# Small tiles of a hybrid block moved to GpSimd's DMA queue, with two kinds of PSUM banks and new latest chunks

## The chip, the cores and the metric

The kernel runs on one core of one Trainium2 chip. The metric is the device time of one execution in microseconds (us); smaller is better. Besides timed runs there is one profiled execution of the kernel, whose trace gives the rows that are shown. In it PE is the matrix engine (TensorE), PEld its weight loads, DVE is VectorE, ACT is ScalarE, POOL is GpSimd and SP is SyncE, which here does nothing but issue DMAs.

## The reference

One layer of a streaming-encoder block on 512 tokens of width 2048, all in f32. The normalised input feeds one wide projection, whose columns go to three branches and to gates; each branch is multiplied by a SiLU gate, projected back to 2048 columns, weighted by a sigmoid gate and summed; a last projection is added to the input.

```python
h = rms_norm(x, norm_g)
p = h @ w_in                       # all branches and gates
A = B * causal_conv3(C * u)        # 1024 channels
M = mla_attention(...)             # 16 heads, low-rank q and kv, rope, chunk mask
X = memory_attention(...)          # 4 heads over 256 memory tokens
A, M, X = A * silu(zA), M * silu(zM), X * silu(zX)
y = sig(gA) * (A @ w_conv_out) + sig(gM) * (M @ w_mla_out) + sig(gX) * (X @ w_mem_out)
return x + y @ w_o
```

## The kernel before

**Precision.** Each f32 operand is split into a rounded part and a remainder, hi and lo (`split`: the rounding is an ACT instruction, L129, the remainder a DVE subtraction, L131). A product is three matmuls, hi·hi, hi·lo and lo·hi (`mm3`, L160 to L162). Every weight is loaded raw (512 KB tiles), split into whi and wlo, and multiplied.

**Chunks.** After the attention of the MLA branch (which ends well before 690 us) the kernel is a written list, `plan`, of 504 chunks, each with one 512 KB weight tile's worth of matmuls (24 matmuls of 5.44 us by the plan's own cost, or 12 matmuls of 2.72 us, or 24 short ones of 2.88 us). The list in order: memory queries (8 chunks), the gate columns memz in two groups of 8, conv (8 groups of 14), mlaz and gconv (4 groups of 14 each), gmem and gmla (2 groups of 28 each), the projection mem_out (16), mla_out (2 groups of 28), the projection conv_out (16), and w_o (2 groups of 28). `plain_group` makes plain chunks; `block_group` and `block_group_t` make chunks of a seven-product scheme, where sums and differences of weight tiles (DVE, L1031, L1116, L1121) and of the tokens (`build`: sums, evens, forms, odds, with costs of 1.26, 0.69, 1.53 and 0.69 us) replace the eighth product. In `block_group_t` the products come in the order P1, P7, P5, P6 (four rounds), then four chunks of P4, then P2 and P3 in turn. The first group of w_o has an order of its own at its start. Results of a block are named "11", "10", "00" and "01".

**Order of work.** `drive` walks over the chunks and emits the instructions of ACT, DVE, PE and POOL in a fixed order: in chunk c first the hooks `at[c]` (mostly loads), then the sums and splits of the weights up to two or three chunks ahead, then the phases, then waiting pieces of work (`todo`), then the chunk's matmuls. A piece has a cost; it is emitted if the cost fits the `room` of DVE left in the chunk (with 0.3 us of grace, or 1.3 in the "patient" chunks, four before w_o and twelve into it), or if it has waited 3 chunks (12 in patient ones), or if its latest chunk, `by`, has come. What a chunk's result needs (`done`) is put into `todo` after its matmuls. Ahead of chunk 0 the order is a scheduler's.

**Buffers.** There are three sets of whi and wlo, so the split of a chunk's weights waits on ACT and DVE for the matmuls of the chunk three before. Raw tiles have four to ten slots. Results of gates and sums, 128x512 f32 (256 KB), live in the tile y, which has four buffers; `when` and `in_turn` load y tiles once one of the four is free by the written order.

**Queues.** SP issues the weight loads (raw: L903, L1070), the loads of the projections' inputs (araw, L1553), those of L1698, and all y loads (`y_tile`, L1212 to L1215, whose DMA is L1214), in one order. An issue that has to wait for a buffer holds up what stands behind it. ACT issues the stores. POOL issues the accumulating DMAs of `conv_result` (`add`, L1674), which add a gated projection (product on DVE, L1677) to a tile of the merged sum.

**PSUM.** The eight banks have four tags, aux0, aux1, acc0 and acc1, of two banks each. `take_pairs` hands out tags from the list `pairs` in turn; a group of four banks takes two tags. The first memz group has the fixed kind acc, so acc0 and acc1 by turns; the second memz group, which follows it, takes the first of the list. A bank can be written again once its result has been read: in memz by an ACT SiLU (L1338) in place and a DVE product (L1341); in mem_out by L1598; in mla_out by L1631 (sums), L1635 (gate), with L1641 (merge) behind it; in the transposes `turn_sums` by copies (L1720).

The steps of the projections: `load(c)` brings araw, `parts_` splits it into the tile act, and `group` makes the chunks and the y loads of the gates.

Of the kernel before, what the change touches and what calls it, by code (L numbers as in the profile page):

```python
# [94 lines left out]
def body(ctx, tc, a, out):  # L95
# [16 lines left out]
    psum = ctx.enter_context(tc.tile_pool(name="ps", bufs=2, space=bass.MemoryType.PSUM))  # L112
# [4 lines left out]
    turns = defaultdict(int)  # L117

    def bank_of(tag):
        return psum.tile([P, 512], F32, tag=tag, name=tag)  # L120

    def bank(tag):

        turns[tag] += 1
        return bank_of(f"{tag}{turns[tag] % 2}")
# [685 lines left out]
    def drive():  # L811
        n, npre, nprep, room = len(plan), 0, 0, 0.0
        for c in range(-3, n + 6):
# [4 lines left out]
            room = min(room, 0.0) + us  # L818
# [68 lines left out]
    def next_banks(n=4, tag=None):  # L887
        if tag is not None:
            return [bank(tag) for _ in range(n)]
        return [bank_of(t) for t in take_pairs(n // 2) for _ in range(2)]  # L890


    def plain_group(src, nch, kc, n, xs, early=4, lead=2, tag=None, mode="F"):


        banks = []
        first = len(plan)
        for c in range(nch):
            hold = {}

            def load(hold=hold, c=c):
                t = take_raw("W")[1].rearrange("p k n -> p (k n)")
                nc.sync.dma_start(t, src[c])  # L903
# [43 lines left out]
    def block_group(src, tokens, consume, loads=(-8, -7, -3, -2), add=None, halves=False):  # L947
# [70 lines left out]
        for n, ch in HALVES_ORDER if halves else PLAIN_ORDER:  # L1018
# [22 lines left out]
                def mm(ch=ch, bn=bn, xn=xn, hold=hold):  # L1041
                    opens = bn not in bk
                    if not bk:
                        bk["pairs"] = take_pairs(2)
                    if opens:
                        bk[bn] = bank_of(bk["pairs"]["XYZW".index(bn) // 2])
# [12 lines left out]
    def block_group_t(src, tokens, results, early=6, opening=()):  # L1059
# [48 lines left out]
        for name, ch in order:  # L1108
# [21 lines left out]
            def mm(name=name, ch=ch, bn=bn, xn=xn, hold=hold):  # L1130
                opens = bn not in bk
                if not bk:

                    bk["pairs"] = take_pairs(4)
                    pairs[:] = [bk["pairs"][i] for i in (3, 1, 0, 2)]
                if opens:
                    bk[bn] = [bank_of(bk["pairs"]["XYZW".index(bn)]) for _ in range(2)]
# [74 lines left out]
    def y_tile(src):  # L1212
        t = pres.tile([P, S], F32, tag="y", name="y", bufs=4)
        nc.sync.dma_start(t, src)  # L1214
# [281 lines left out]
    def gate_rows(n0, grp):  # L1496
# [3 lines left out]
        def results(name, o, i0, i1):  # L1500
# [23 lines left out]
            out_ = [(0, 0 if i1 is None else 0.69, piece(lambda tb=tb: made(tb), by=first + 29)) for tb in range(2)]  # L1524
# [15 lines left out]
    for n, nm in ((0, "w_gmem"), (2, "w_gmla")):  # L1540
        for grp in range(2):
            block_group_t(a[nm][grp], tx, gate_rows(16 * n, grp))


    def projection(weights_, n0, gate, result, halves=None, gates=None, mode="F"):
# [25 lines left out]
        def group(src, nch, kc, n, j):  # L1571
            g0, banks = plain_group(src, nch, kc, n, lambda k: acts[k], early=3, mode=mode)
# [12 lines left out]
        for grp in range(4):  # L1585
            if grp < 3 or halves is None:
                group(weights_[grp], 4, KC, 512, 4 * grp)
            else:
                for i in range(2):
                    group(halves[i], 2, 4, HS, 12 + 2 * i)  # L1590
# [3 lines left out]
    def mem_result(j, b, sg):  # L1594
# [3 lines left out]
        return [(0, 0.69, piece(lambda: vec.tensor_tensor(out=sg(), in0=b(), in1=sg(), op=ALU.mult), sg)),  # L1598
# [14 lines left out]
    def mla_rows(grp):  # L1613
# [3 lines left out]
        def load(name, tb, k):  # L1617
            ys[name, tb, k] = y_tile((mdram if k else gdram[32:])[rows(grp, name, tb)])
# [4 lines left out]
        def results(name, o, i0, i1):  # L1623
            y = lambda tb, k: (lambda: ys.get((name, tb, k)))
            end = first + {"11": 20, "10": 28, "00": 29, "01": 30}[name]
            inx = o is not None
            out_ = []
            for tb in range(2):
# [25 lines left out]
            return out_ + [(3, 0, lambda tb=tb: store(tb)) for tb in range(2)]  # L1654
        return results

    for grp in range(2):
        block_group_t(a["w_mla_out"][grp], ta, mla_rows(grp), 6 if grp else 5)
# [29 lines left out]
    def turn_sums(n):  # L1688
# [41 lines left out]
    def out_group(grp, early):  # L1730
# [54 lines left out]
        block_group_t(a["w_o"][grp], to, results, early, () if grp else opening)  # L1785
# [107 lines left out]
```

## Time and profile before

| what | us |
|---|---|
| median of three timed runs | 2211.35 (2210.38 to 2215.31) |
| the profiled execution's own time | 2208.95 |
| its span in the profile | 2207.2 |
| PE busy | 2138.1 (97%) |
| DVE busy | 1574.5 (71%) |
| ACT busy | 1031.1 (47%) |
| POOL busy | 181.3 (8%) |

The span runs from the first to the last instruction of the trace. A row of a view names a line of the kernel, an engine, an operation and its tiles as "out<-in". PE is pipelined, and its busy time says nothing of its clock; the granted clock is listed by window as a share of full speed. The DMA engines moved 323.93 MB at a mean of 147 GB/s; the hardware queues are listed as q1 and q10, and the queue on which POOL's DMAs run as q0, with 8.39 MB.

### The profile page before, as it was taken

How to read it: one execution, taken by the hardware profiler on the slowest of the kernel's cores; microseconds unless marked ns; L12 is line 12 of the kernel's file. 1: busy time of each engine (PE TensorE's matmuls, PEld its weight loads, DVE VectorE, ACT ScalarE, POOL GpSimd, SP SyncE). 2: the span in 40 equal slices, each digit the busy share in tenths (PEclk: the TensorE clock that was granted, in tenths of full speed). 3: DMA queues.
4: the chain of work that ended last, by engine and by line, in shares of the span. 5: the costliest groups of instructions: out<-in, count | busy, mean ns of one | idle time of the engine just before them, and what ended most of it. 6: DMA issues, size and time to landing. Idle time of an engine off the chain costs nothing.

```text
span 2207.2 us, 31861 instructions
## 1 busy us (share of the span) xinstructions
PE 2138.1 (97%) x12504; PEld 1896.5 (86%) x12504; DVE 1574.5 (71%) x2194; ACT 1031.1 (47%) x1551; POOL 181.3 (8%) x157
## 2 busy tenths in 40 slices
PE   7999999999999999999999999999999999989899
PEld 5788888887778999999999999888888878878687
DVE  7853767774335887787777767777776779846887
ACT  5532677674333444444444544445444433424433
POOL 7510312220001000000000000000000000001000
PEclk9999999999999999999999999999999999999999
DMA  7473212134227523423345334335335746478352
GB/s 261 161 254 109 78 57 74 63 130 156 83 77 236 206 89 106 139 97 105 129 147 194 133 116 153 105 134 172 135 102 203 251 169 201 155 242 252 105 200 96
DMA packets 116103, 323.93 MB, mean 147 GB/s; under 512 B 13296, under 2 KB 13552, under 8 KB 115952
## 3 DMA queue, kind: packets, MB, share of 16 engines
q1 hardware_dynamic: 90000, 274.87, 36.6%
q10 hardware_dynamic: 21600, 38.63, 4.6%
q0 software_dynamic: 4352, 8.39, 2.0%
q8 instruction: 98, 1.61, 0.3%
q14 instruction: 53, 0.43, 0.1%
HBM read 269.41 MB, written 48.23 MB: 144 GB/s over the span
## 4 chain that ended last, share of the span: by engine, by line
PE 88%; DVE 5%; DMA 2%; ACT 2%; issue 2%; POOL 1%; ACTq 0%; SPq 0%; DVEq 0%; POOLq 0%
PE acc L161 16%; PE acc L160 16%; PE acc L162 16%; PE aux L161 12%; PE aux L160 12%; PE aux L162 12%; DVE wlo L154 1%; PE aux L211 1%; DVE wlo L131 1%; PE aux L667 1%; DMA raw<-in_w_conv_out 1%; ACT whi L129 1%; POOL xs L311 1%; PE aux L647 0%; PE aux L649 0%
## 5 line engine op out<-in xcount | busy, mean ns | idle before, releaser
L131 DVE TENSOR_TENSOR wlo<-raw,whi 128x1024 fp32r<-128x1024 f32 x440 | 538.4, 1224 | 377.5 <-ACT whi L129 364.6
L129 ACT ACTIVATE whi<-raw 128x1024 fp32r<-128x1024 f32 x440 | 465.9, 1060 | 689.0 <-PE acc L161 188.5
L154 DVE TENSOR_TENSOR wlo<-raw,whi 128x1024 fp32r<-128x1024 f32 (+3 forms) x97 | 119.1, 1229 | 105.3 <-ACT whi L153 104.1
L153 ACT ACTIVATE whi<-raw 128x1024 fp32r<-128x1024 f32 (+3 forms) x97 | 92.4, 953 | 124.9 <-PE acc L162 49.7
L160 PE MATMUL acc<-whi,blk 128*128 128x512 f32 (+1 forms) x320 | 120.7, 381 | 7.3 <-ACT blk L129 5.3
L161 PE MATMUL acc<-wlo,blk 128*128 128x512 f32 (+1 forms) x320 | 119.7, 375 | 2.4 <-DVE wlo L131 1.5
L1674 POOL DMA_DIRECT2D hU<-y x14 | 12.5, 1281 | 1312.7 <-DVE y L1677 1295.4
L160 PE MATMUL acc<-blk,whi 128*128 128x256 f32 (+1 forms) x352 | 112.1, 319 | 8.0 <-ACT sq L1231 8.0
L162 PE MATMUL acc<-whi,blk 128*128 128x512 f32 (+1 forms) x320 | 119.3, 374 | 0.0
L1121 DVE TENSOR_TENSOR raw<-raw 128x1024 f32<-128x1024 f32 x96 | 117.1, 1220 | 0.0
L1031 DVE TENSOR_TENSOR raw<-raw 128x1024 f32<-128x1024 f32 x96 | 117.0, 1219 | 0.0
L160 PE MATMUL acc<-whi,f 128*128 128x512 f32 x288 | 112.6, 391 | 0.5 <-DVE u L1631 0.5
L161 PE MATMUL acc<-wlo,f 128*128 128x512 f32 x288 | 112.6, 391 | 0.0
L162 PE MATMUL acc<-whi,f 128*128 128x512 f32 x288 | 112.4, 390 | 0.0
L161 PE MATMUL acc<-blk,whi 128*128 128x256 f32 (+1 forms) x352 | 111.3, 316 | 0.6 <-DVE blk L131 0.6
L129 ACT ACTIVATE whi<-s 128x1024 fp32r<-128x1024 f32 x64 | 67.9, 1061 | 93.8 <-PE aux L161 21.1
L162 PE MATMUL acc<-blk,wlo 128*128 128x256 f32 (+1 forms) x352 | 110.5, 315 | 0.0
L160 PE MATMUL acc<-hU,whi 128*128 128x256 f32 (+1 forms) x352 | 110.0, 312 | 0.0
L161 PE MATMUL acc<-hU,whi 128*128 128x256 f32 (+1 forms) x352 | 109.8, 312 | 0.0
L162 PE MATMUL acc<-hU,wlo 128*128 128x256 f32 (+1 forms) x352 | 109.5, 312 | 0.0
L160 PE MATMUL acc<-f,whi 128*128 128x256 f32 x384 | 108.7, 283 | 0.0
L161 PE MATMUL acc<-f,whi 128*128 128x256 f32 x384 | 108.7, 283 | 0.0
(425 smaller groups left out, 6267.5 us busy)
## 6 DMA issues: line engine op xcount, KB each, us to landing
raw<-in_w_conv SPq DMA_DIRECT2D x64, 512.0 KB, 4.5
raw<-in_w_mlaz SPq DMA_DIRECT2D x32, 512.0 KB, 4.9
raw<-in_w_gconv SPq DMA_DIRECT2D x32, 512.0 KB, 4.3
raw<-in_w_gmem SPq DMA_DIRECT2D x32, 512.0 KB, 3.6
raw<-in_w_gmla SPq DMA_DIRECT2D x32, 512.0 KB, 3.3
raw<-in_w_mla_out SPq DMA_DIRECT2D x32, 512.0 KB, 6.1
raw<-in_w_o SPq DMA_DIRECT2D x32, 512.0 KB, 6.2
raw<-in_w_mem_kv SPq DMA_DIRECT2D x31, 512.0 KB, 3.3
```

Source lines behind the costliest of these rows:

```text
L129: act.activation(hi, src, AF.Copy, scale=1.0 if g is None else g)
L131: vec.tensor_tensor(out=lo, in0=src, in1=r32(hi), op=ALU.subtract)
L153: act.activation(hi[:, cols], raw[:, cols], AF.Copy)
L154: vec.tensor_tensor(out=lo[:, cols], in0=raw[:, cols], in1=r32(hi[:, cols]), op=ALU.subtract)
L160: nc.tensor.matmul(o, lhsT=s[0], rhs=m[0], start=start, stop=False, skip_group_check=shared)
L161: nc.tensor.matmul(o, lhsT=s[0], rhs=m[1], start=False, stop=False, skip_group_check=shared)
L162: nc.tensor.matmul(o, lhsT=s[1], rhs=m[0], start=False, stop=stop, skip_group_check=shared)
L211: nc.tensor.transpose(out=b[:, i * P:(i + 1) * P], in_=s, identity=ident)
L311: pool.tensor_tensor(out=xs, in0=xraws[k // KC][:, k % KC], in1=scale, op=ALU.mult)
L667: nc.tensor.transpose(out=b[:, i * P:(i + 1) * P], in_=ps[i][:, j * P:(j + 1) * P], identity=ident)
L1031: vec.tensor_tensor(out=o, in0=i0, in1=i1, op=op)
L1121: vec.tensor_tensor(out=o, in0=i0, in1=i1, op=op)
```

## The change

1. y loads of the projections' gates, of mla_out and of the residual input in w_o (80 loads in all) are issued by `pool`, GpSimd's queue. The y loads of memz and mlaz (24) stay on SP.
2. PSUM has two tags, aux and acc, with four banks each. `next_tag` alternates between them and returns the tag and the other one; `again` and `turn` say where a group does not, or does once more, move the turn on. `turn_sums` takes the kind that comes next. memz's first group keeps the fixed tag acc.
3. Latest chunks: the sums of `gate_rows` are due at 27 ("00") or 28 instead of 29; the splits of the projections' inputs get a latest chunk; the last four gates of mem_out get one in the first two chunks after it; in mla_out "00" is due at 27 instead of 29 and "01" at 28 instead of 30, with the "01" gate and merge three chunks later than before and its stores at 6 instead of 3.
4. In patient chunks the room for pieces is 8% larger.

```diff
-    psum = ctx.enter_context(tc.tile_pool(name="ps", bufs=2, space=bass.MemoryType.PSUM))
+    psum = ctx.enter_context(tc.tile_pool(name="ps", bufs=4, space=bass.MemoryType.PSUM))
...
-            room = min(room, 0.0) + us
+            room = min(room, 0.0) + us * (1.08 if c in patient else 1.0)
...
-    pairs = ["aux0", "aux1", "acc0", "acc1"]
-
-    def take_pairs(n):
-
-        t = pairs[:n]
-        pairs[:] = pairs[n:] + t
-        return t
...
+    tags = [0]
+
+    def next_tag():
+        tags[0] += 1
+        return ("aux", "acc")[tags[0] % 2], ("acc", "aux")[tags[0] % 2]
...
-                    banks.extend(next_banks(n // P if mode == "F" else NTB, tag))
+                    t = tag or (next_tag()[0] if turn else ("aux", "acc")[tags[0] % 2])
+                    banks.extend(bank(t) for _ in range(n // P if mode == "F" else NTB))
...
-                        bk["pairs"] = take_pairs(2)
+                        bk["tag"] = next_tag()[0]
...
-                    bk["pairs"] = take_pairs(4)
-                    pairs[:] = [bk["pairs"][i] for i in (3, 1, 0, 2)]
+                    t, o = next_tag()
+                    bk["tags"] = dict(zip("XWYZ", (t, t, o, o)))
+                    if not again:
+                        tags[0] += 1
...
-    def y_tile(src):
+    def y_tile(src, eng=nc.sync):
         t = pres.tile([P, S], F32, tag="y", name="y", bufs=4)
-        nc.sync.dma_start(t, src)
+        eng.dma_start(t, src)
         return t
...
-            out_ = [(0, 0 if i1 is None else 0.69, piece(lambda tb=tb: made(tb), by=first + 29)) for tb in range(2)]
+            out_ = [(0, 0 if i1 is None else 0.69, piece(lambda tb=tb: made(tb), by=first + (27 if name == "00" else 28))) for tb in range(2)]
...
-                    lambda n=KC * c + k: later(0, 0.69, piece(lambda: parts_(n), lambda: raws.get(n // KC))))
+                    lambda n=KC * c + k: later(0, 0.69, piece(lambda: parts_(n), lambda: raws.get(n // KC),
+                                                              by=first + n // KC - 1)))
...
-                when(c, "y", lambda i=i: sgs.append(y_tile(gdram[gate + j + i])))
+                when(c, "y", lambda i=i: sgs.append(y_tile(gdram[gate + j + i], pool)))
...
-        return [(0, 0.69, piece(lambda: vec.tensor_tensor(out=sg(), in0=b(), in1=sg(), op=ALU.mult), sg)),
+        by = dict(by=len(plan) + (j - 12) // 2) if j >= 12 else {}
+        return [(0, 0.69, piece(lambda: vec.tensor_tensor(out=sg(), in0=b(), in1=sg(), op=ALU.mult), sg, **by)),
...
-            end = first + {"11": 20, "10": 28, "00": 29, "01": 30}[name]
+            end = first + {"11": 20, "10": 28, "00": 27, "01": 28}[name]
...
-                out_ += [(0, 0.69, piece(gate, y(tb, 0), **({} if inx else dict(by=end)))),
-                         (0, 0.69, piece(merge, y(tb, 1)))]
+                d = 3 if name == "01" else 0
+                out_ += [(d, 0.69, piece(gate, y(tb, 0), **({} if inx else dict(by=end)))),
+                         (d, 0.69, piece(merge, y(tb, 1)))]
...
-            return out_ + [(3, 0, lambda tb=tb: store(tb)) for tb in range(2)]
+            return out_ + [(6 if name == "01" else 3, 0, lambda tb=tb: store(tb)) for tb in range(2)]
...
-            spot = 1 if n == 3 else 0
+            t = ("aux", "acc")[(tags[0] + 1) % 2]
             for f in range(4):
-                b = bank_of(pairs[spot + f // 2])
+                b = bank(t)
...
-            xs[name, tb] = y_tile(a["xrow"][2 * t + tb][:, 1024 * grp + 512 * n:1024 * grp + 512 * (n + 1)])
+            xs[name, tb] = y_tile(a["xrow"][2 * t + tb][:, 1024 * grp + 512 * n:1024 * grp + 512 * (n + 1)], pool)
```

More of the change, by code (lines that the diff above doesn't have):

```diff
@@ L876, in parts_tile, with plain_group @@
         return hi, lo
-    pairs = ["aux0", "aux1", "acc0", "acc1"]
-    def take_pairs(n):
-        t = pairs[:n]
-        pairs[:] = pairs[n:] + t
-        return t
[L887 to L893, printed above, removed]
+    tags = [0]
+    def next_tag():
+        tags[0] += 1
+        return ("aux", "acc")[tags[0] % 2], ("acc", "aux")[tags[0] % 2]
+    def plain_group(src, nch, kc, n, xs, early=4, lead=2, tag=None, mode="F", turn=True):
         banks = []
@@ L1043, in mm @@
                     if not bk:
-                        bk["pairs"] = take_pairs(2)
+                        bk["tag"] = next_tag()[0]
                     if opens:
-                        bk[bn] = bank_of(bk["pairs"]["XYZW".index(bn) // 2])
+                        bk[bn] = bank(bk["tag"])
                     hi, lo = hold["w"]
@@ L1132, in mm @@
                 if not bk:
-                    bk["pairs"] = take_pairs(4)
-                    pairs[:] = [bk["pairs"][i] for i in (3, 1, 0, 2)]
+                    t, o = next_tag()
+                    bk["tags"] = dict(zip("XWYZ", (t, t, o, o)))
+                    if not again:
+                        tags[0] += 1
                 if opens:
-                    bk[bn] = [bank_of(bk["pairs"]["XYZW".index(bn)]) for _ in range(2)]
+                    bk[bn] = [bank(bk["tags"][bn]) for _ in range(2)]
                 last = name in ("P2", "P3", "P4", "P6")
@@ L1568, in projection, with group @@
                 at[first + (-2, -1, 1, 2)[c]].append(
[L1569 to L1572 removed]
+                    lambda n=KC * c + k: later(0, 0.69, piece(lambda: parts_(n), lambda: raws.get(n // KC),
+                                                              by=first + n // KC - 1)))
+        def group(src, nch, kc, n, j, turn=True):
+            g0, banks = plain_group(src, nch, kc, n, lambda k: acts[k], early=3, mode=mode, turn=turn)
             sgs = []
@@ L1589, in projection @@
                 for i in range(2):
-                    group(halves[i], 2, 4, HS, 12 + 2 * i)
+                    group(halves[i], 2, 4, HS, 12 + 2 * i, i == 0)
         return first
@@ L1617, in load @@
         def load(name, tb, k):
-            ys[name, tb, k] = y_tile((mdram if k else gdram[32:])[rows(grp, name, tb)])
+            ys[name, tb, k] = y_tile((mdram if k else gdram[32:])[rows(grp, name, tb)], pool)
         in_turn("y", [(first + c, lambda name=name, tb=tb, k=k: load(name, tb, k))
```

14 lines of the change are left out of this document (5 added, 9 removed).

## The prediction

> **What bounds the kernel now.** I read the head of the page first. The matrix engine is busy nearly all the time, so only two things can move the end: stretches in which it stands still, and stretches in which it runs at a lower clock.
>
> ```profile
> span 2207.2 us, 31861 instructions
> ```
>
> Busy time, share and count of each engine:
>
> ```profile
> PE 2138.1 (97%) x12504; PEld 1896.5 (86%) x12504; DVE 1574.5 (71%) x2194; ACT 1031.1 (47%) x1551; POOL 181.3 (8%) x157
> ```
>
> The sum below is made against this execution, whose time outside the profiler's span was 2208.95 us. The median of the three timed runs is 2211.35, 2.4 above it, and I add those 2.4 at the end.
>
> Second, the waits of the matrix engine from 690 us to the end, where all stages that the diff reorders lie. Columns: who waits and for which line, total us, times, longest.
>
> ```profile
> PE acc L160 <- ACT blk L129: 5.3, 1, 5.3
> PE acc L161 <- DVE act L131: 3.6, 2, 2.2
> PE acc L160 <- ACT act L129: 3.3, 2, 1.8
> PE aux L160 <- DVE y L1598: 3.1, 1, 3.1
> PE acc L161 <- DVE wlo L131: 1.5, 1, 1.5
> PE acc L160 <- ACT whi L129: 0.6, 1, 0.6
> PE acc L161 <- DVE blk L131: 0.6, 1, 0.6
> PE acc L160 <- DVE u L1631: 0.5, 1, 0.5
> PE acc L1706 <- DVE y L1677: 0.4, 1, 0.4
> PE acc L160 <- DVE y L1598: 0.4, 1, 0.4
> PE aux L160 <- DVE y L1635: 0.4, 1, 0.4
> ```
>
> They add to 19.7 us. That is the whole stock of waits from which the change can gain after 690 us. Third, busy time by window shows what a wait costs beyond itself. Columns: window, length, busy (count) of PE, PEld, DVE, ACT, POOL, then granted clock, share of the DMA engines, GB/s.
>
> ```profile
> 1500.00:1550.00 50.00, 50.00 (x223) 41.39 (x222) 40.22 (x40) 23.45 (x26) 0.00 (x0) 1.00 0.56 184
> 1776.00:1788.00 12.00, 8.42 (x36) 6.36 (x35) 9.38 (x10) 3.14 (x3) 0.00 (x0) 1.00 0.36 145
> 1845.00:1880.00 35.00, 34.03 (x148) 27.13 (x147) 31.71 (x33) 12.74 (x12) 0.00 (x0) 1.00 0.75 254
> 1931.00:1960.00 29.00, 22.10 (x76) 16.68 (x75) 15.34 (x21) 7.37 (x11) 0.00 (x0) 0.82 0.91 315
> 2039.00:2059.00 20.00, 17.81 (x76) 13.90 (x75) 19.90 (x25) 8.67 (x12) 3.53 (x4) 1.00 0.57 158
> 2075.00:2090.00 15.00, 9.65 (x30) 7.32 (x29) 10.09 (x17) 7.82 (x13) 0.00 (x0) 0.77 0.10 35
> ```
>
> The first is the undisturbed pace: 223 matmuls in 50 us, 4.46 per us. Lost time of a window is its length less count/4.46: 3.9, 1.8, 12.0, 3.0 and 8.3 us. At 1776 the loss is the waits alone (3.1 + 0.4), at full clock. At 2075 it is 5.3 of wait and 2.9 more, with the clock at 0.77; at 1931 it is 6.9 of wait (3.6 + 3.3) and 5.1 more, at 0.82. So a stop of 5.3 us, or two close together, carries some 2.6 to 2.9 us of half speed with it; one of 3.1 does not.
>
> **A: the second memz group.** Before, the first group of w_memz takes the fixed tag acc, the second the first pairs of the list, aux0 and aux1. After, the counter of next_tag starts at 0 and is raised to 1, which gives acc: the four banks that the first group has just filled. In the matmul timeline the second group went on without a stop:
>
> ```profile
> 691.80 0.39 PE L160 MATMUL aux<-blk,whi 128*128 128x512 f32 x1
> ```
>
> Before a bank can be reused, its SiLU (L1338) and the gate after it (L1341) must have read it. ACT has two weight splits and a table load ahead of the SiLU:
>
> ```profile
> 691.77 2.01 ACT L129 ACTIVATE whi<-raw 128x1024 fp32r<-128x1024 f32 x2 [4.38 <-PE acc L161]
> 693.80 1.28 ACT L1338 ACT_TABLE_LOAD   x1
> 695.10 2.05 ACT L1338 ACTIVATE acc<-acc 128x512 f32<-128x512 f32 x4
> ```
>
> ```profile
> 695.71 2.48 DVE L1341 TENSOR_TENSOR y<-acc,y 128x512 f32<-128x512 f32 x4 [0.48 <-ACT acc L1338]
> ```
>
> The first gate ends at 695.71 + 2.48/4 = 696.3, so the matmul that began at 691.80 begins at 696.4: 4.5 us lost. The other three banks come 0.6 us apart, faster than the group uses them. Nothing hides this: nothing ahead of the SiLU waits for the stopped matmuls, and the queue's order is written out. Half speed: 4.5 lies between the 3.1 that had none and the 5.3 that had 2.9, nearer the latter, and I take 2.0 for it. **+6.5**, bounds +3.9 and +7.4.
>
> The Trainium skill ("TensorE: Matmul & The Clock Gate", What's actually happening) says that a free-running window of about 3.4 us without work halves the clock until a busy window has passed. The two rows at 0.77 and 0.82 agree; by that rule the term would be 4.5 + 2.9 = 7.4.
>
> **B: mem_out to mla_out.** The last gates of mem_out (L1598) stand behind a weight split on DVE, which itself waits for the matmuls to give up their set of split weights:
>
> ```profile
> 1783.21 1.22 DVE L131 TENSOR_TENSOR wlo<-s,whi 128x1024 fp32r<-128x1024 f32 x1 [0.33 <-ACT whi L129]
> 1784.35 1.28 DVE L1598 TENSOR_TENSOR y<-aux,y 128x512 f32<-128x512 f32 x2
> ```
>
> After, pieces 12 to 15 have a latest chunk at the first two chunks of mla_out. The gates then come ahead of these splits; 3.1 + 0.4 is there, a split delayed by a gate may take 0.3 back. **−3.2**, bounds −3.5 and 0.
>
> **C: first to second mla_out group** (1845 to 1880, lost 1.8; waits 0.5 on L1631 and 0.4 on L1635). The gate of "00" is due two chunks sooner. **−0.8**, bounds −1.8 and +1 (a gate that now waits for its tile).
>
> **D: start of conv_out** (1931 to 1960, lost 12.0). SP issues everything in one order, and its y loads wait for merges and stores before their buffers are free. What is queued behind them are the tiles of the projection:
>
> ```profile
> 1921.66 2.38 SPq L1214 DMA_DIRECT2D y<-gdram  x2
> ```
>
> and then
>
> ```profile
> 1930.89 2.13 SPq L1214 DMA_DIRECT2D y<-mdram  x2
> 1933.12 0.38 SPq L903 DMA_DIRECT2D raw<-in_w_conv_out  x1
> 1933.60 0.85 SPq L1553 DMA_DIRECT2D araw<-adram  x2
> ```
>
> araw of 1933.60 feeds the splits for which the matmuls wait. With the y loads on GpSimd's queue it can be issued once its raw slot is free, many us sooner. The parts_ pieces get a latest chunk too. Both kinds of wait (6.9) and the half speed (5.1) should go, but the DMA engines are at 0.91 here, and the move creates no bandwidth: I leave 2.5 standing. **−9.5**, bounds −12 and 0.
>
> The Trainium skill ("DMA: Bandwidth & Descriptors", Issuing engines are not separate DMA queues) says that another issuing engine saves only sequencer time. The row at 1921.66 is a blocked sequencer, which that rule does not price; by it alone D would be near 0, the third rival below.
>
> **E: turn_sums** (L1706 waits 0.4 for a bank): **−0.5**, bounds −1.2 and +1.
>
> **F: start of w_o** (0.6 + 1.5 of waits, lost 3.0 at 2039). Its first raw tiles are behind y loads that wait for L1674's adds; the first split came only then:
>
> ```profile
> 2024.11 1.79 SPq L1214 DMA_DIRECT2D y<-gdram  x2
> 2025.99 2.42 SPq L1070 DMA_DIRECT2D raw<-in_w_o  x3
> ```
>
> ```profile
> 2032.31 1.06 ACT L129 ACTIVATE whi<-raw 128x1024 fp32r<-128x1024 f32 x1 [8.90 <-DMA raw<-in_w_o]
> ```
>
> After, they can be issued earlier; but DVE is busy 19.90 of 20 us from 2039, so a head start is partly used up. **−1.8**, bounds −3.0 and 0.
>
> **G: chunk 12 of w_o** (5.3 of wait, 8.3 lost at 2075). The matmuls want the parts of the last block, which DVE splits at the last moment:
>
> ```profile
> 2080.84 0.69 DVE L131 TENSOR_TENSOR blk<-eo,blk 128x512 fp32r<-128x512 f32 x1 [0.36 <-ACT blk L129]
> ```
>
> Room grows by 8% in the 16 patient chunks: four of 5.44 us and twelve of 2.72 us give 54.4 us, so 4.4 us more. The builds are pieces of 1.26, 0.69, 1.53 and 0.69; 4.4 is one build. Counting room chunk by chunk, the split of the last evens moves from chunk 12 to about chunk 10; the forms stay at 12 and are wanted at 13, so about 3 us of stop remains, perhaps without half speed. **−4.5**, bounds −8.3 and +1.
>
> **H: up to 690 us.** The four tags become two of four banks. Waits for banks there:
>
> ```profile
> PE aux L211 <- DVE ptl L131: 5.9, 4, 2.0
> PE aux L647 <- DVE mx L654: 2.5, 2, 1.4
> ```
>
> Four banks in one turn can free these 8.4 or, in another order, lengthen them. **−1**, bounds −8.4 and +5.
>
> **The new queue itself.** 80 loads (32 gates of the projections, 32 of mla_out, 16 of w_o) leave SP. GpSimd has no compute in the windows at 1500, 1776, 1845, 1931 and 2075; only L1674's accumulating DMAs share it. They are the nearest rows for a price:
>
> ```profile
> L1674 POOL DMA_DIRECT2D hU<-y x14: 869/1175/1798, 1976.1 to 2042.8; - x14
> ```
>
> ```profile
> DMA to landing us min/median/max: 3.2/4.5/7.1
> ```
>
> The y loads on SP, on the same view of L1214, land in:
>
> ```profile
> DMA to landing us min/median/max: 2.5/4.3/11.3
> ```
>
> An issue costs GpSimd about 0.9 to 1.8 us, 80 of them 70 to 144 us on an engine idle there; landing is about as before. In conv_out the adds wait for L1677's products, and y loads queue behind them, as they did behind the buffers on SP: no new wait. At the end the last x tiles may land up to 7.1 − 2.5 = 4.6 later: **+0.5**, bounds 0 and +4.6.
>
> Edits that cost nothing: the "01" gate, merge and store three chunks later (these chunks have DVE room in the 1845 window, 31.71 of 35; without it a split is pushed by 0.69 each), and the parity flags, which only choose banks.
>
> **Sum.** 6.5 − 3.2 − 0.8 − 9.5 − 0.5 − 1.8 − 4.5 − 1 + 0.5 = −14.3. The profiled time would be 2194.7, the median 2194.7 + 2.4 = 2197.
>
> **The rivals.**
>
> *Everything closes.* B 3.5, C 1.8, D 12, F 3, G 8.3, H 1, with A at 3.9: −25.7, or 2186. For it: each wait has a release that the diff moves. Against: DVE has no room at 2039, and A is a plain loss.
>
> *DVE keeps F and G.* At 19.90 of 20 busy, 8% more assumed room delays splits instead. F 0, G 0, the rest as above: −8.0, or 2203. For it: that row. Against: DVE waited before 2033 for the tiles of w_o, and that idle time can be filled.
>
> *The transfers, not the queue, are late.* 0.91 of the DMA engines at 315 GB/s: loads issued sooner land no sooner. D −3, B −3.2, C, F, G and E nothing, A +6.5: about 0, or 2211. Against: the window before is not as full, 0.75 at 1845, so earlier issue has somewhere to go.
>
> *Slower: the gates of "00" wait for their tiles.* In mla_out they are now due two chunks (2 x 2.72 = 5.4 us) sooner. The first of them at the second end ran here:
>
> ```profile
> 1935.32 0.68 DVE L1635 TENSOR_TENSOR y<-aux,y 128x512 f32<-128x512 f32 x1
> ```
>
> so its turn would come at about 1930. Its tiles were issued from 1921.66 to 1924.0, after the merges that free the buffers. With an issue of 1.8 and a landing of 7.1 they land at 1933, DVE sleeps 3 to 4 us, and the weight splits of the next chunks, queued behind it, hold the matmuls. Price: 3.7 of stop and 2.9 of half speed at each of the two ends of mla_out, 13.2; D's gain is lost as well, C too. 13.2 + 6.5 − 3.2 − 0.5 − 1.8 − 4.5 − 1 + 0.5 = +9.2, or 2221. It decides from landings of about 5 us on.
>
> A rule of the Trainium skill would make this likelier ("SBUF — State Buffer", SBUF: two separate sides): descriptors of a DMA from GpSimd are written by GpSimd, and DVE operations that take the shared port pair lock it out; it measured 620 ns growing to 3100. The adds of L1674 at 869 ns, among DVE work that fills its window, do not show that, so I keep the chance low.
>
> **How the numbers follow.** Forecast 50%, by itself 2190 to 2204; everything closes 12%; DVE keeps F and G 13%; transfers 14%; slower 11%. A measurement of this kernel tells about 0.2%, 4.4 us, from no change. Faster: 0.50 + 0.12 + 0.13 = 0.75; same 0.14; slower 0.11. Half of the outer cases is left out at each end: 2185 to 2212, from "everything closes" to the transfers' case.
>
> **What would show it.** A: a wait of some 4.5 us on L1341 near 692. B: no wait on L1598. D: no y loads among SP's issues at 1920 to 1935, and the waits on act gone. F: the first split of w_o before 2030. G: the wait on blk at 3 or less. The queue: landings of y at 4 to 5 us. I am wrong if A doesn't appear, if new waits on L1635 or L1641 do, or if GpSimd's landings pass 7 us.

## The result and the profile after

The changed kernel takes 2188.94 us (median of four runs, 2188.3 to 2189.58) against 2213.02 for the kernel before (four runs, 2210.38 to 2215.31): a ratio of 0.9892, 95% interval 0.9874 to 0.9909, or 24.1 us less. The profiled executions are 19.4 apart (2189.56 against 2208.95), because the profiled run of before lies 4 us under its median and that of after does not. The terms below are compared with the 19.4.

Lines have moved in the new file: the split is L122 (ACT) and L124 (DVE), the three matmuls are L153 to L155, memz's gate is L1330, mla_out's gate and merge are L1627 and L1633, the y loads L1203, the adds L1667. First the head of the page after:

```profile
span 2187.8 us, 31886 instructions
...
PE 2134.7 (98%) x12504; PEld 1897.0 (87%) x12504; DVE 1574.7 (72%) x2194; ACT 1028.0 (47%) x1551; POOL 222.0 (10%) x237
```

Then the waits of PE from 640 us to the end, in the columns of the prediction:

```profile
PE acc L154 <- DVE wlo L124: 6.0, 2, 5.6
PE acc L153 <- DVE y L1330: 4.5, 1, 4.5
PE aux L154 <- DVE blk L124: 0.6, 1, 0.6
PE acc L155 <- DVE f L124: 0.6, 1, 0.6
PE aux L154 <- DVE act L124: 0.5, 1, 0.5
PE aux L153 <- DVE y L1590: 0.4, 1, 0.4
```

Of the waits before, all above 0.6 us are gone, and two that were not there have come: 4.5 us for memz's gate, which was forecast, and 5.6 us for a weight split at 2037, which was not. The windows around the places of the prediction (clock, DMA share and GB/s are the last three columns):

```profile
686.00:700.00 14.00, 9.74 (x33) 7.86 (x34) 5.71 (x7) 5.98 (x8) 4.14 (x5) 0.76 1.10 264
1920.00:1950.00 30.00, 29.51 (x138) 23.90 (x137) 19.66 (x24) 13.54 (x19) 3.33 (x7) 1.00 0.92 311
2026.00:2046.00 20.00, 14.39 (x58) 11.45 (x57) 14.24 (x17) 5.82 (x6) 3.98 (x6) 0.91 0.64 151
2055.00:2080.00 25.00, 24.41 (x107) 19.83 (x107) 21.95 (x27) 13.78 (x18) 0.00 (x0) 1.00 0.31 106
```

At 4.46 matmuls per us the first has lost 6.6 us, with the clock at 0.76; conv_out's start (second row) loses nothing, at the same DMA share as before, which speaks against the rival that held the transfers to be late; the start of w_o (third) loses 7.0 where it lost 3.0; the place of the old 8.3 us (fourth) loses 1.0.

To divide the 19.4 us I compared the start of the same weight split, the n-th of 601 on DVE, in both traces. Where the difference changes, time was won or lost (the n-th of the 12504 matmuls gives the same within 0.1):

| step | forecast | measured |
|---|---|---|
| H, up to 690 us | −1 | −6.2 |
| A, second memz group | +6.5 | +7.0 |
| B, mem_out to mla_out | −3.2 | −3.4 |
| C, between the mla_out groups | −0.8 | −1.2 |
| D, start of conv_out | −9.5 | −11.3 |
| E, transposes | −0.5 | −1.1 |
| F and G, w_o | −6.3 | −3.2 |
| queue at the end | +0.5 | 0.0 |

### The profile page after: what moved, and what is told of

It is laid out like the page before. It is cut to its first block, busy times and chain, and to the rows that moved or that the text cites. A ratio compares the mean times of both kernels' runs of the same rounds, so it can differ in the third digit from the quotient of the medians.

```text
span 2187.8 us, 31886 instructions
## 1 busy us (share of the span) xinstructions
PE 2134.7 (98%) x12504; PEld 1897.0 (87%) x12504; DVE 1574.7 (72%) x2194; ACT 1028.0 (47%) x1551; POOL 222.0 (10%) x237
## 5 line engine op out<-in xcount | busy, mean ns | idle before, releaser
L124 DVE TENSOR_TENSOR wlo<-raw,whi 128x1024 fp32r<-128x1024 f32 x440 | 538.2, 1223 | 360.0 <-ACT whi L122 351.3
L122 ACT ACTIVATE whi<-raw 128x1024 fp32r<-128x1024 f32 x440 | 466.2, 1060 | 683.3 <-PE acc L154 196.2
L1203 POOL DMA_DIRECT2D y<-gdram x48 | 26.4, 550 | 1195.9 <-DMA gdram<-gy 959.5
L153 PE MATMUL acc<-blk,whi 128*128 128x256 f32 (+1 forms) x384 | 126.7, 330 | 11.5 <-ACT sq L1220 7.0
L153 PE MATMUL acc<-whi,blk 128*128 128x512 f32 (+1 forms) x352 | 133.1, 381 | 2.1 <-DVE qt L585 1.4
L155 PE MATMUL acc<-whi,blk 128*128 128x512 f32 (+1 forms) x352 | 131.9, 375 | 0.0
L154 PE MATMUL acc<-wlo,blk 128*128 128x512 f32 (+1 forms) x352 | 131.5, 374 | 0.0
L154 PE MATMUL acc<-blk,whi 128*128 128x256 f32 (+1 forms) x384 | 125.4, 327 | 0.0
L155 PE MATMUL acc<-blk,wlo 128*128 128x256 f32 (+1 forms) x384 | 124.5, 326 | 0.0
L153 PE MATMUL acc<-hU,whi 128*128 128x256 f32 (+1 forms) x384 | 122.5, 319 | 0.0
L154 PE MATMUL acc<-hU,whi 128*128 128x256 f32 (+1 forms) x384 | 122.2, 318 | 0.0
L155 PE MATMUL acc<-hU,wlo 128*128 128x256 f32 (+1 forms) x384 | 121.9, 318 | 0.0
L122 ACT ACTIVATE whi<-s 128x1024 fp32r<-128x1024 f32 x64 | 67.9, 1062 | 103.9 <-PE aux L155 21.5
L153 PE MATMUL aux<-f,whi 128*128 128x256 f32 x384 | 108.7, 283 | 0.0
L154 PE MATMUL aux<-f,whi 128*128 128x256 f32 x384 | 108.7, 283 | 0.0
L155 PE MATMUL aux<-f,wlo 128*128 128x256 f32 x384 | 108.7, 283 | 0.0
L153 PE MATMUL acc<-f,whi 128*128 128x256 f32 x384 | 108.7, 283 | 0.0
```

Source lines behind the costliest of these rows:

```text
L122: act.activation(hi, src, AF.Copy, scale=1.0 if g is None else g)
L124: vec.tensor_tensor(out=lo, in0=src, in1=r32(hi), op=ALU.subtract)
L153: nc.tensor.matmul(o, lhsT=s[0], rhs=m[0], start=start, stop=False, skip_group_check=shared)
L154: nc.tensor.matmul(o, lhsT=s[0], rhs=m[1], start=False, stop=False, skip_group_check=shared)
L155: nc.tensor.matmul(o, lhsT=s[1], rhs=m[0], start=False, stop=stop, skip_group_check=shared)
L1203: eng.dma_start(t, src)
```

## The experiments

Every ratio is to the kernel before, timed on the same chip. `e5` and `e12` are edits of the kernel before, `e11` is an edit of `e9`, and all others are edits of the changed kernel (2188.94). Executions with the same order of work differ by up to 4.5 us at 690 us already, so places are compared in the traces, by the n-th matmul or split, and small differences of medians are not read.

**y loads back on SP** (`e1`).

```diff
     def y_tile(src, eng=nc.sync):
...
-        eng.dma_start(t, src)
+        nc.sync.dma_start(t, src)
```

> The changed kernel with one part undone: all y loads are again issued by SP; banks, latest chunks and the 8% stay. Theory (the blocked SP queue made the stop at the start of conv_out): the waits on act come back, about 11 us, while the start of w_o gets cheaper by some 4 because its raw loads are issued later and no longer compete with the accumulating adds: about 2196. Rival (banks and latest chunks closed that gap, the queue did nothing): within 2 us of the changed kernel, 2187 to 2191.

Measured: 2191.17 us (2187.66 to 2194.09), ratio to before 0.9897 (0.9882 to 0.9911). This is nearer to the rival than to the theory. The waits of PE in its trace, rows two to four:

```profile
PE aux L153 <- DVE y L1627: 1.9, 1, 1.9
PE aux L154 <- DVE wlo L124: 1.6, 1, 1.6
PE aux L1699 <- DVE y L1670: 1.4, 1, 1.4
```

By the n-th matmul the start of conv_out got 2.3 us worse and the transposes behind it 2.1, not 11, and w_o about 1 better. So most of D did not come from the queue, against the prediction's step: with all y loads on SP the other edits still close 8.9 of its 11.2.

**The second memz group on aux** (`e2`).

```diff
-    tags = [0]
+    tags = [1]
```

> The changed kernel with the counter of next_tag started at 1 instead of 0, so that the second memz group takes aux and every later group the other kind than before. Theory (the 4.5 us wait on L1330 near 690 and the half clock after it are caused by the shared kind alone): the wait goes, 7 us less, 2182. Rival (the stop only moves to the next group or is a wait on ACT's order): 2187 to 2190.

Measured: 2183.95 us (2179.37 to 2186.62), ratio 0.9864 (0.9846 to 0.9883). By the n-th matmul 7.0 us go near 690 and none comes back. The wait on L1330 is gone, and the largest one left is:

```profile
PE aux L154 <- DVE wlo L124: 6.1, 2, 5.5
```

A is shown: one shared kind of bank cost 4.5 us of stop and 2.5 of half clock.

**Without the 8%** (`e3`).

```diff
-            room = min(room, 0.0) + us * (1.08 if c in patient else 1.0)
+            room = min(room, 0.0) + us
```

> The changed kernel without the 8% more room in patient chunks. Theory (the 8% removed the stop at chunk 12 of w_o, 8 us, but put the sums of block 6 ahead of the weight sums at chunk 0, where they wait for an add that lands after 9.8 us: 5.6 of stop and 1.5 of half clock): the stop at 2037 goes and the one at chunk 12 comes back, so the two cancel: 2188 to 2191. Rival as the prediction had it (the 8% is a gain of 4.5 and the stop at 2037 is due to DVE having no time): 2193 to 2194, with the stop at 2037 still there.

Measured: 2190.44 us (2187.72 to 2191.64), ratio 0.9892 (0.9878 to 0.9907): no difference from the changed kernel that can be told. Its waits of PE:

```profile
PE aux L153 <- ACT blk L122: 5.3, 1, 5.3
PE acc L153 <- DVE y L1330: 4.5, 1, 4.5
PE aux L154 <- DVE wlo L124: 1.1, 1, 1.1
```

The old stop at chunk 12 is back in full and the new one at 2037 is gone. The 8% moved a stop from one place to another.

**Block 6 later** (`e4`).

```diff
-    TIMES, FORMS = (5, 5, 8, 8, 12, 12, 14, 16), (7, 7, 10, 10, 14, 14, 16, 20)
+    TIMES, FORMS = (5, 5, 8, 8, 12, 12, 14, 16), (7, 7, 10, 10, 14, 14, 18, 20)
```

This is FORMS, the delays after which the forms of each block of the last projection may be emitted.

> The changed kernel with the forms of block 6 asked for two chunks later (18 instead of 16 in FORMS): on DVE the three sums of that block move behind three weight sums and three splits, nothing else changes place by more. Theory (DVE slept for the landing of the add, with the weight sums queued behind it): the wait on wlo near 2037 falls from 5.6 to under 2, no half clock, and chunk 12 stays without a stop: 2183 to 2185. Rival (the raw tiles of w_o themselves land too late, or DVE is full): the wait stays above 3.5, 2187 to 2190.

Measured: 2182.94 us (2181.57 to 2184.35), ratio 0.986 (0.9846 to 0.9875). Why the order mattered is seen in the DVE timeline of the changed kernel:

```profile
2026.52 1.22 DVE L124 TENSOR_TENSOR wlo<-raw,whi 128x1024 fp32r<-128x1024 f32 x1
2033.46 0.43 DVE L1174 TENSOR_TENSOR t<-hU 128x256 f32<-128x256 f32 x1 [5.73 <-DMA hU<-y]
...
2034.60 1.22 DVE L1103 TENSOR_TENSOR s<-raw 128x1024 f32<-128x1024 f32 x1
2035.73 1.22 DVE L124 TENSOR_TENSOR wlo<-s,whi 128x1024 fp32r<-128x1024 f32 x1
```

DVE slept 5.73 us for an add into hU, with the weight sum and split that the matmuls needed standing behind it. GpSimd had issued that pair of adds at 2023; SP had issued six 512 KB loads for w_o just before and beside it:

```profile
2023.00 1.85 POOL L1667 DMA_DIRECT2D hU<-y  x2 [8.34 <-DVE t L1186]
```

```profile
2016.92 6.57 SPq L1057 DMA_DIRECT2D raw<-in_w_o  x6
```

The landing of all adds in that kernel (least, median, most) was

```profile
DMA to landing us min/median/max: 3.3/5.0/9.8
```

against 3.2/4.5/7.1 before; the 9.8 is the second add of that pair. In the ten runs with y loads on GpSimd's queue the slowest add took 8.9 to 9.8, in the four without it 7.1 to 8.4. With the sums three weight splits later the waits of PE begin with memz's and then

```profile
PE acc L155 <- DVE f L124: 1.9, 1, 1.9
```

The stop of 5.6 is gone, and 1.9 comes in its place, at 2058. By the n-th matmul 7.2 us go at the old stop and 3.0 come back at the new one, which has half clock behind it, so w_o is 4.3 shorter.

**The queue alone** (`e5`): the kernel before with `pool` as the queue of the three groups of y loads.

```diff
-    def y_tile(src):
+    def y_tile(src, eng=nc.sync):
...
-        nc.sync.dma_start(t, src)
+        eng.dma_start(t, src)
...
-                when(c, "y", lambda i=i: sgs.append(y_tile(gdram[gate + j + i])))
+                when(c, "y", lambda i=i: sgs.append(y_tile(gdram[gate + j + i], pool)))
...
-            ys[name, tb, k] = y_tile((mdram if k else gdram[32:])[rows(grp, name, tb)])
+            ys[name, tb, k] = y_tile((mdram if k else gdram[32:])[rows(grp, name, tb)], pool)
...
-            xs[name, tb] = y_tile(a["xrow"][2 * t + tb][:, 1024 * grp + 512 * n:1024 * grp + 512 * (n + 1)])
+            xs[name, tb] = y_tile(a["xrow"][2 * t + tb][:, 1024 * grp + 512 * n:1024 * grp + 512 * (n + 1)], pool)
```

> The kernel before with one part of the change: the y loads of the projections, of mla_out and of w_o on GpSimd's queue; banks, latest chunks and room as before. First theory (the prediction's: the queue alone opens the start of conv_out): the waits on act fall from 6.9 to under 2, 10 us less or more: about 2201 to 2203. Second theory (after the run with y on SP: the order of work on DVE, set by banks and latest chunks, does most of it, and the queue some 4 to 5): the splits of act still stand behind merges that wait for their tiles, waits on act of 3 or more, 2206 to 2210.

Measured: 2210.52 us (2207.01 to 2213.79), ratio 0.9989 (0.9979 to 0.9998), about 2.7 us less by the medians. The one trace of each says 2.3 more (6.2 lost near 1880 and 0.4 at conv_out, 1.1 won in the transposes and 3.0 in w_o), and the trace of before is a quick execution. The first theory falls either way; the second has the waits right and a gain of the queue that is not seen. Waits of PE:

```profile
PE acc L161 <- DVE act L131: 5.8, 2, 5.3
PE acc L160 <- ACT blk L129: 5.3, 1, 5.3
PE aux L161 <- DVE wlo L131: 4.0, 1, 4.0
PE acc L160 <- ACT act L129: 3.3, 1, 3.3
```

The waits on act are 9.1 where they were 6.9, and a new one of 4.0 stands at 1880. DVE's timeline at the start of conv_out shows why in this run:

```profile
1953.01 0.69 DVE L1641 TENSOR_TENSOR u<-u,y 128x512 f32<-128x512 f32 x1 [4.18 <-DMA y<-mdram]
...
1957.64 2.49 DVE L131 TENSOR_TENSOR act<-araw,act 128x512 fp32r<-128x512 f32 x4
```

The merge of "01" waits for its tile, whose load waits for a free y buffer, and the splits of act stand behind that merge in DVE's written order. The same sleep is there at 1877:

```profile
1877.78 0.69 DVE L1641 TENSOR_TENSOR u<-u,y 128x512 f32<-128x512 f32 x1 [4.10 <-DMA y<-mdram]
```

All araw tiles had landed by 1949.6, eight us before these last splits. In the kernel before they were not late either. The araw loads of conv_out's start landed there in

```profile
DMA to landing us min/median/max: 4.6/5.3/6.1
```

so those of 1933.60, which the prediction took for late, were there by 1940.6 at the latest, and their splits ran ten us later, ACT's behind a weight split that had waited 8.01 for the matmuls, DVE's behind a merge of "01" that waits for its tile, as in `e5` but for less:

```profile
1949.42 1.06 ACT L129 ACTIVATE whi<-raw 128x1024 fp32r<-128x1024 f32 x1 [8.01 <-PE acc L161]
1950.39 2.17 ACT L129 ACTIVATE act<-araw 128x512 fp32r<-128x512 f32 x4
```

```profile
1947.79 0.69 DVE L1641 TENSOR_TENSOR u<-u,y 128x512 f32<-128x512 f32 x1 [2.42 <-DMA y<-mdram]
```

**Banks and the dates that free them** (`e6`): the changed kernel without the queue, without the 8% and without the dates of `parts_`.

```diff
-        eng.dma_start(t, src)
+        nc.sync.dma_start(t, src)
...
-            room = min(room, 0.0) + us * (1.08 if c in patient else 1.0)
+            room = min(room, 0.0) + us
...
-                    lambda n=KC * c + k: later(0, 0.69, piece(lambda: parts_(n), lambda: raws.get(n // KC),
-                                                              by=first + n // KC - 1)))
+                    lambda n=KC * c + k: later(0, 0.69, piece(lambda: parts_(n), lambda: raws.get(n // KC))))
```

> The changed kernel without GpSimd's queue, without the 8%, and without the latest chunks of the splits of the projections' inputs: what is left are the banks of two kinds and the latest chunks that free banks. First theory: memz +7, the part up to 690 us -6, mem_out to mla_out -3.4, the two mla groups -1.2, start of conv_out as before: 2213 - 3.6 = 2209. Second theory (banks and their latest chunks alone reorder DVE so that the start of conv_out loses 6 less): 2202 to 2204.

Measured: 2201.14 us (2196.28 to 2204.29), ratio 0.994 (0.9916 to 0.9964). The second theory is the nearer one. The trace is of the slowest of the four runs; it agrees with the changed kernel's within 0.3 us up to 1680, so H and A belong to the banks; B and C are there too. At the start of conv_out it loses 7.6 more than the changed kernel and 3.6 less than the kernel before, where the theory had 6, by these waits:

```profile
PE aux L154 <- DVE act L124: 3.2, 1, 3.2
PE aux L154 <- DVE wlo L124: 2.3, 2, 1.6
PE aux L153 <- DVE y L1626: 1.7, 1, 1.7
```

In H the wait of one line has shrunk most. After, in the waits up to 690 us:

```profile
PE aux L204 <- DVE ptl L124: 0.9, 1, 0.9
```

It was 5.9 (the same line, L211, of before); 4.1 of that lay between 395 and 500 us, where 4.7 us were won. Why four banks in turn spare it was not tried by itself.

**Without the dates of parts_** (`e7`): the last hunk of `e6` alone.

> The changed kernel without the latest chunks of the splits of the projections' inputs (parts_). If these dates closed the start of conv_out: the waits on act come back by 3 to 5 us, 2192 to 2195. If not (banks or the dates of mla_out did): as the changed kernel, 2187 to 2190.

Measured: 2192.47 us (2192.07 to 2193.23), ratio 0.9909 (0.9892 to 0.9925): 3.5 us back, within what the first case named; by the n-th matmul 3.0 of it at the start of conv_out. The wait that returns is 1.7 longer, not 3 to 5, and has half clock behind it:

```profile
PE aux L154 <- DVE act L124: 2.2, 1, 2.2
```

**Without the dates of mla_out** (`e8`).

```diff
-            end = first + {"11": 20, "10": 28, "00": 27, "01": 28}[name]
+            end = first + {"11": 20, "10": 28, "00": 29, "01": 30}[name]
...
-                d = 3 if name == "01" else 0
+                d = 0
...
-            return out_ + [(6 if name == "01" else 3, 0, lambda tb=tb: store(tb)) for tb in range(2)]
+            return out_ + [(3, 0, lambda tb=tb: store(tb)) for tb in range(2)]
```

> The changed kernel with the dates of mla_out as before ("00" due at 29, "01" at 30, its gate, merge and store not later). DVE then has a merge ahead of the splits of act at the start of conv_out. If this order was the cause of the stop there: 3 to 6 us back, and 1 at the middle of mla_out, where banks come later: 2193 to 2196. If not: only the 1 us, 2188 to 2191.

Measured: 2195.44 us (2195.19 to 2197.54), ratio 0.9924 (0.9907 to 0.9941): 6.5 back. The time is that of the first case, the place is not: by the n-th matmul 6.9 are lost near 1870, where 1 was expected, and 2.0 at the start of conv_out, where 3 to 6 were; up to 690 us this execution happened to be 4 us shorter. Waits of PE, rows three and four:

```profile
PE aux L154 <- DVE wlo L124: 4.4, 2, 4.2
PE aux L153 <- DVE y L1627: 2.7, 1, 2.7
```

and DVE before the first of them:

```profile
1871.57 0.69 DVE L1633 TENSOR_TENSOR u<-u,y 128x512 f32<-128x512 f32 x1 [4.42 <-DMA y<-mdram]
```

It is the sleep of `e5` again.

**Both edits** (`e9`): `tags = [1]` and FORMS with 18.

> The changed kernel with both edits that helped: the second memz group on aux, and the forms of block 6 two chunks later. Theory (two separate stops, 690 and 2037): the gains add, 2176 to 2178, with only waits below 2 us left after 640. Rival (they share something, for instance the place of the later stops): 2181 or more.

Measured: 2174.91 us (2173.91 to 2175.12), ratio 0.9831 (0.9817 to 0.9846). It beats both kernels, 38 us under the one before and 14.0 under the changed one, and 1.1 below the range expected. The rival falls: the gains do not share anything, they come to more than the sum of the two alone (5.0 and 6.0 by the medians; 7.0 and 4.3 of 14.4 by the n-th matmul, since of the 3.0 that came back in `e4` only 1.2 come back here). The two longest waits of PE from 640 us on:

```profile
PE aux L155 <- DVE f L124: 1.3, 1, 1.3
PE acc L154 <- DVE blk L124: 0.6, 1, 0.6
```

**"01" not later** (`e10`): the changed kernel with `d = 0` in place of `d = 3 if name == "01" else 0`.

> The changed kernel with the gate and merge of "01" in mla_out not three chunks later (all other dates as changed). Theory (this delay is what covers the tiles that come over GpSimd's queue): DVE sleeps some 4 us for y<-mdram with weight splits behind it, at the start of the second mla_out group and again at the start of conv_out; 5 to 7 us back, 2194 to 2196. Rival (the earlier date of "00" was what mattered): 2188 to 2191.

Measured: 2193.07 us (2190.68 to 2194.24), ratio 0.9913 (0.9897 to 0.9929), between the two cases. One stop comes back, at 1873, worth 3.8 by the n-th matmul, and none at conv_out:

```profile
PE aux L154 <- DVE wlo L124: 2.6, 1, 2.6
```

So in the changed kernel the delay of "01" covers a part of the middle of mla_out, worth about 4, and conv_out's start does without it. The rest of what `e8` lost belongs to the earlier dates of "00" and "01" or to the later stores, which were not tried apart.

**The best version with y on SP** (`e11`): `e9` with the edit of `e1`.

> The version with aux for memz and block 6 later, with all y loads on SP again. Theory (once the order on DVE is right, the queue is worth what the start of conv_out and the start of w_o show, some 4 and 2): 2181 to 2184. Rival (the queue is worth nothing any more): 2176 to 2179.

Measured: 2182.7 us (2181.65 to 2188.65), ratio 0.9877 (0.9859 to 0.9895). The queue is worth 7.8 us here, where it was worth 2.2 in the changed kernel. By the n-th matmul it gives about the same in both at the start of conv_out and in the transposes (4.6 and 4.4 in all); at w_o it gives 3.4 here and cost 1 there, where block 6 waited for the slow add. The first weight load of w_o is issued at 1980.6 in `e9` and at 2005.7 in `e11`, behind y loads that wait for buffers. What returns without it:

```profile
PE acc L154 <- DVE wlo L124: 1.5, 1, 1.5
PE acc L153 <- DVE y L1627: 1.4, 1, 1.4
```

**Queue and "01" later, on the kernel before** (`e12`): `e5` with

```diff
-                out_ += [(0, 0.69, piece(gate, y(tb, 0), **({} if inx else dict(by=end)))),
-                         (0, 0.69, piece(merge, y(tb, 1)))]
+                d = 3 if name == "01" else 0
+                out_ += [(d, 0.69, piece(gate, y(tb, 0), **({} if inx else dict(by=end)))),
+                         (d, 0.69, piece(merge, y(tb, 1)))]
...
-            return out_ + [(3, 0, lambda tb=tb: store(tb)) for tb in range(2)]
+            return out_ + [(6 if name == "01" else 3, 0, lambda tb=tb: store(tb)) for tb in range(2)]
```

> The kernel before with the queue and, in mla_out, gate and merge of "01" three chunks later (stores six); banks and all else as before. Theory (queue and delay belong together): of the run with the queue alone the stops at 1880 (4.0 and half clock) and on act (9.1 and half clock) go for the most part: 2195 to 2199. Rival (banks of two kinds are needed too): 2204 or more.

Measured: 2198.26 us (2196.85 to 2199.87), ratio 0.9938 (0.9922 to 0.9954). That is the theory's range. By the n-th matmul, against the queue alone, 11.1 us go at the start of conv_out and 6.0 near 1880; of the waits on act there is left

```profile
PE acc L161 <- DVE act L131: 1.3, 1, 1.3
```

The merge still sleeps, and longer than before, but the splits of act now stand ahead of it:

```profile
1949.28 1.29 DVE L131 TENSOR_TENSOR act<-araw,act 128x512 fp32r<-128x512 f32 x2
...
1958.34 0.69 DVE L1641 TENSOR_TENSOR u<-u,y 128x512 f32<-128x512 f32 x1 [4.60 <-DMA y<-mdram]
```

By the medians the queue gave 2.7, and 14.5 with this one delay (2.3 lost and 12.1 won in the traces). Neither the banks nor the other dates are needed for that. Whether the queue is needed is not shown: the delay without it was not run.

## Why the prediction was right or wrong

The time lay in the stated range and the sign was right; the size was 24.1 where 14.3 was forecast, 19.4 by the profiled runs. At 2188.94 the time lies below the 2190 to 2204 that the forecast had for itself, and nearer to the rival "everything closes" (2186), which is not what happened: a new stop opened at F. Of the 5.1 between 14.3 and 19.4, H alone makes 5.2; the misses of the other terms cancel, which is luck.

**A** was right in cause and size: 4.5 of stop, half clock after it, 7.0 by the split, and `e2` removes it. Half clock took 2.5, so the value of 2.0 was low. That a stop of 3.1 carries no half clock does not hold in general; the last section has the rows.

**B** and **C** came out within 0.4.

**D** had the right size by a step that did not carry it, and that is luck. "araw of 1933.60 feeds the splits for which the matmuls wait" took the transfer for late; the tiles lay ready for ten us, and what was late was the place of the splits in the written order of ACT and DVE. The weights of conv_out are the transfer that ACT does wait for there, and it waits for them as long in the changed kernel (9.1 us in both, from 1915 to 1958). "With the y loads on GpSimd's queue it can be issued ... many us sooner" is true of the queue's order and alone brings nothing there (`e5`). Two ways of changing the order did: the later "01" on top of the queue (`e12`, 11.1 us at this place), and the banks and dates with all loads on SP (`e1`, 8.9 of 11.2, of which the banks and the dates of mla_out make 3.6, `e6`).

**"Edits that cost nothing: the '01' gate, merge and store three chunks later"** was wrong: put at nothing, that edit is worth 4 in the changed kernel (`e10`) and is what made the queue pay in `e12`. The slower rival had the mechanism, DVE asleep for a y tile with weight splits behind it, for the gates of "00"; the runs show it for the merges of "01" (4.10 and 4.18 in `e5`), and the change had moved them out of the way. Its price of 3.7 and 2.9 of half clock for a stop was close: 6.9 in `e8`, and 3.8 where the delay alone is undone (`e10`).

**F** had the wrong sign. "They can be issued earlier" was right and had a price that I did not see: the loads of w_o were issued ahead of and beside the last adds, whose landing grew to 9.8 us, and the 8% had put the sums that need them ahead of the weight sums. 3.0 lost became 7.0. Without the 8% the earlier issue does what F said: the start of w_o loses nothing in `e3`.

**G** was undersized: 7.3 instead of 4.5 gone, no stop of 3 us left. Over w_o the 8% is nevertheless worth nothing (`e3`), since F's loss is its other side. The rival "DVE keeps F and G" fails too, with its reason: DVE was busy 14.24 of the 20 us in which F's stop lies, so it was not full, it slept, and in `e3` it is busy all of the same 20 us and the matmuls lose nothing.

**H** was the largest error of size, −6.2 for −1, inside its bounds. In the eleven traces with the changed kernel's order up to 690 us it comes to 5.0 to 8.8. I took a small value because the order there is a scheduler's; the row of 5.9 us for one wait was the better guide.

**The new queue** was priced well in time, 0.0 for 0.5. An issue of a y load cost GpSimd 0.55 us, not 0.9 to 1.8. In the changed kernel the 80 y loads from GpSimd landed in

```profile
DMA to landing us min/median/max: 2.8/4.6/8.4
```

against 2.5/4.3/11.3 for all 104 from SP before. The prediction named three signs of being wrong. A came, no new wait on L1635 or L1641 did, but GpSimd's landings passed 7 us: 8.4 for a y load, 9.8 for an add, and the add is where F failed. The locked port that the Trainium skill describes ("SBUF — State Buffer", SBUF: two separate sides) does not show in the landings of y. The Trainium skill's rule on issuing engines ("DMA: Bandwidth & Descriptors", Issuing engines are not separate DMA queues), that another engine saves only sequencer time and usually little, does not fit in size: 7.8 us between `e9` and `e11`, by sequencer time that was a blocked wait.

The timed runs of the kernel before spread over some 9 us in all comparisons (2208.84 to 2218.32), the four of the changed kernel over 1.3 and the four of `e9` over 1.2, but those of `e2` and `e11` over 7. One part of it shows in the traces: in the eleven executions whose order of work up to 690 us is the changed kernel's, the matmul after the same 3.53 us wait starts between 621.8 and 625.5. Why stays open. The 4.7 between 19.4 and 24.1 are the distances of the two profiled executions from their medians (4.1 and 0.6).

## What to carry to other kernels

Before you call a transfer late, compare its landing with the start of the instruction that uses it, and follow it through the queue of that engine: an earlier issue is worth nothing while the consumer's in-order queue has something else asleep in front. Move a queue and the pieces that wait for its tiles in one change, and test each alone and both together: here 2.7 became 14.5, and the delay alone is the run that is missing. When loads are set free, look at which small transfers they overtake, and put the work that waits for those behind work that is ready.

## What the runs showed that was not expected

An accumulating DMA of 256 KB that landed in 7.1 us at most before landed in 9.8 when six loads of 512 KB had been issued in the 7 us around it, though the DMA engines were not full in that stretch (0.76, 215 GB/s):

```profile
2016.00:2034.00 18.00, 15.39 (x68) 12.40 (x67) 11.31 (x20) 6.29 (x10) 1.85 (x2) 1.00 0.76 215
```

That those loads delayed it is argued from the order of issues; the add was not run without them. A room 8% larger left the total the same, with a stop of 5.3 us exchanged for one of 5.6. A stop of 4.5 us cost 7.0 with the half clock behind it, and taking it away gave all 7.0 back, with no stop elsewhere in its place.

Whether a short stop is followed by half clock is not settled by its length. The stop of 3.15 us on L1598 is the same in the kernel before and in `e12`, and the 5 us behind it are, in this order,

```profile
1785.00:1790.00 5.00, 4.82 (x21) 4.03 (x22) 2.40 (x4) 1.06 (x1) 0.00 (x0) 1.00 0.18 70
1784.70:1789.70 5.00, 4.83 (x14) 3.87 (x15) 1.75 (x3) 0.46 (x1) 0.00 (x0) 0.66 0.00 0
```

with 1.00 of the clock in the first and 0.66 in the second. In `e4` a stop of 1.9 had it too (0.73 from 2060 to 2065). From 640 us on every stop of 4 us or more in these traces had it.
